# A two-layer decoder trunk on one core: half-size tiles for lone weight splits, and feed-forward down products accumulated onto the residual in PSUM

## The chip, the cores and the metric

The kernel runs on one core of one Trainium2 chip. The metric is the device time of one execution in microseconds (us). Three runs of the kernel before gave 2322.97, 2323.41 and 2323.65 us; the median is 2323.41 us.

## The reference, cut to what matters

The model is a trunk of two layers on 256 tokens of width 2048, in float32. Each layer has a token mixer beside a cross-attention, an output projection, and a SwiGLU feed-forward part (FFN) of inner width 5632. The change touches the FFN, the way in which weights are split for every projection, and the transposes.

```python
def ffn_part(h, layer):
    hn = _rmsnorm(h, norm_ffn[layer])
    gate, up = jnp.split(hn @ w_gate_up[layer], 2, axis=-1)
    h = h + (jax.nn.silu(gate) * up) @ w_down[layer]
    return h
```

## The kernel before, in words

Every float32 matrix product is made of three passes with rounded operands: each operand is split into a high part and a rest, and high x high, high x rest and rest x high are added in one PSUM bank. So every weight that arrives must be split by two instructions: ScalarE casts the high part (L207), VectorE subtracts it from the weight to get the rest (L208). `split` makes both, into a tile `parts` that holds two k-slices of 512 columns with their rests. There are six such tiles. The weights land in tiles `raw` of four slices of 128x512 (1 MB); there are four of these, given out in turn, so the load of `raw` number i waits until the last reader of number i-4 is through. All loads of weights are issued from SyncE's queue, in order.

Up and gate projection (`project_halves`, L321 to L372): the FFN width is worked off in 11 blocks of 512 columns. A block is made of eight pieces, each with one `raw` tile (two loads of 512 KB: columns of gate and of up). Most pieces (kind S) are a Strassen-like step: seven products in place of eight, for which VectorE forms sums of weight slices in place in `raw` (L350, L351, L352) before they are split. Kind S makes four splits: `a` is one slice alone, `b`, `c` and `d` are two slices each; `c` needs L350, `d` needs L351 and L352. Kind O makes two splits, `a` and `b`, of two slices each. From the fourth block of a layer the kinds are S S O S S O S S. The products of a block collect in seven of the eight PSUM banks, and VectorE adds these up (L833) and makes the gated value (L836).

Down projection (`down`, L843 to L853, with `project`, L220 to L254): blocks in pairs (the first alone) are multiplied with `w_down`, in four pieces of 512 output columns each; two such pieces are made behind each block, while the remainder of the queue `todo` waits. A down piece has one PSUM bank for each half of the tokens, and at its end `add_h` (L410 to L414) lets VectorE add both banks onto the residual `h`: two instructions, L414. The last part (blocks 9 and 10) follows at the layer's end with other work behind it.

The order of the instructions on each engine is fixed when the program is built, by a scheduler that starts from the order in the source, from free buffers and from its own estimate of durations. Each engine then works its list in order. The profile names weight tiles by their running number: pieces 160 to 167 are the eight pieces of block 7 in layer 0, and 156 to 159 are the down weights before them.

Of the kernel before, what the change touches and what calls it, by code (L numbers as in the profile page):

```python
# [35 lines left out]
def trunk_kernel(ctx: ExitStack, tc: tile.TileContext, x, mem, norm_mix, norm_ffn, norm_mem,  # L36
# [118 lines left out]
    def transposes(srcs, name):  # L155

        ps = aux_ps(name)
        for k, src in enumerate(srcs):
            for t in range(NT):
                nc.tensor.transpose(out=ps[:, k * T + t * P:k * T + (t + 1) * P], in_=src(t), identity=ident)  # L160
        return ps

    def make_quad(quad, src, gains, same=False):

# [31 lines left out]
    def new_raw():  # L196
        i = n_w[0]
        n_w[0] += 1
        return i, wts.tile([P, 4, 512], F32, tag="raw", name=f"raw{i}", bufs=4)

    def split(src, name, by=2):

        n, m = src.shape[1:]
        both = wts.tile([P, 2, 2, 512], F32R, tag="parts", name=f"parts{name}", bufs=6)
        for k in range(0, n, by):
            j = min(k + by, n)
            nc.scalar.copy(out=both[:, 0, k:j, 0:m], in_=src[:, k:j, :])  # L207
            nc.vector.tensor_tensor(out=both[:, 1, k:j, 0:m], in0=src[:, k:j, :],  # L208
                                    in1=both[:, 0, k:j, 0:m].bitcast(F32), op=ALU.subtract)
        return [(both[:, 0, k, 0:m], both[:, 1, k, 0:m]) for k in range(n)]  # L210
# [6 lines left out]
                              in_=w[(k0 + j) * P:(k0 + j + m) * P, c0:c0 + n].rearrange("(k p) c -> p k c", p=P))  # L217
        return [p for k in range(0, nk, 2) for p in split(raw[:, k:k + 2, 0:n], f"{i}_{k}", 1 if i == 0 else 2)]

    def project(quads, order, w, c0, n, name, parts=None, prep=None, by_tile=None):  # L220

        parts = parts or [(0, n)]
        ps = [[mm_ps(f"{name}_{i}_{t}") for t in range(NT)] for i in range(len(parts))]
        if by_tile is None:
            groups = [([qi], range(NT)) for qi in range(len(order))]
        else:
            groups = [(range(len(order)), [t]) for t in range(NT)]  # L230
        got = {}
        for qis, ts in groups:
            for qi in qis:
                q = order[qi]
                if prep:
                    prep(q)
                if qi not in got:
                    got[qi] = weights(w, 4 * q, 4, c0, n)
                for k, (hi, lo) in enumerate(got[qi]):
                    if k == 2 or (k == 0 and qi > 0):  # L240
                        step()
                    first = qi == 0 and k == 0
                    last = qi == len(order) - 1 and k == 3
                    for t in ts:
                        xh = quads[q].h[:, k, t * P:(t + 1) * P]
                        xl = quads[q].l[:, k, t * P:(t + 1) * P]
                        for i, (o, m) in enumerate(parts):
                            acc = ps[i][t][:, 0:m]
                            nc.tensor.matmul(acc, xh, hi[:, o:o + m], start=first, stop=False)  # L249
                            nc.tensor.matmul(acc, xh, lo[:, o:o + m], start=False, stop=False)  # L250
                            nc.tensor.matmul(acc, xl, hi[:, o:o + m], start=False, stop=last)  # L251
            if by_tile is not None:
                by_tile(ts[0], ps[0][ts[0]])
        return ps if len(parts) > 1 else ps[0]  # L254
# [66 lines left out]
    def project_halves(forms, kinds, w, c0, c1, name):  # L321
# [15 lines left out]
        for p, kind in enumerate(kinds):  # L337
# [4 lines left out]
                                  in_=w[2 * p * P:(2 * p + 2) * P, c:c + 512].rearrange("(k p) c -> p k c", p=P))  # L342
            x = forms[p].get
            last = p == len(PAIRS) - 1
            if kind == "S":
                tt = nc.vector.tensor_tensor
                b00, = split(raw[:, 0:1, :], f"{i}a")
                b11, b10 = split(raw[:, 2:4, :], f"{i}b")

                tt(out=raw[:, 0:2, :], in0=raw[:, 0:4:2, :], in1=raw[:, 1:2, :].broadcast_to([P, 2, 512]), op=ALU.subtract)  # L350
                tt(out=raw[:, 2, :], in0=raw[:, 2, :], in1=raw[:, 0, :], op=ALU.add)  # L351
# [36 lines left out]
    def h_forms(forms, n, gain, ss, name):  # L388

        for t in range(NT):  # L390
            square_sum(h[:, t, n * 512:(n + 1) * 512], ss[:, t, n:n + 1], f"{name}{n}{t}")

        def turn(p):
            forms[p] = Forms(p, f"{name}{p}")
            ps = aux_ps(f"tp_{name}{p}")
            for i, (t, k) in enumerate(((1, 0), (0, 0), (0, 1), (1, 1))):
                c = (2 * p + k) * P
                nc.tensor.transpose(out=ps[:, i * P:(i + 1) * P], in_=h[:, t, c:c + P], identity=ident)
            forms[p].put(ps, [gain[:, 2 * p + k:2 * p + k + 1] for k in range(2)])

        later(lambda: turn(2 * n), lambda: turn(2 * n + 1))
# [420 lines left out]
    def ffn(l, forms, r, after, tail=None):  # L822
# [21 lines left out]
        def down(i, n):  # L844
            end = i == len(PARTS) - 1
            if end and n == NQ - 1 and tail:
                flush()
                project(sq, PARTS[i], w_down[l], 512 * n, 512, f"fd{l}_{i}_{n}", by_tile=tail)
                return
            ps = project(sq, PARTS[i], w_down[l], 512 * n, 512, f"fd{l}_{i}_{n}")  # L850
            add_h(ps, 512 * n, 512)
            if end:
                after(n)  # L853

        todo = []
        for b in range(DFF // 512):
# [101 lines left out]
```

## Time and profile before

| | |
|---|---|
| median of three runs | 2323.41 us |
| the profiled execution's own time | 2322.12 us |
| its span, first to last instruction | 2320.3 us |
| TensorE busy (modelled ends) | 2297.6 us, 99% |
| VectorE busy | 1887.7 us, 81% |
| ScalarE busy | 1261.2 us, 54% |
| weights and other data read | 430.48 MB |

The shares are averages over stages. In the mixers (the first 520 us, and again from about 1220 to 1600 us) VectorE is busy 50 to 70% of the time; in the two FFN stages it is busy 99%. Matmuls overlap in this profile, and their ends are modelled, so TensorE's busy share says little; the spacing of their starts tells more.

### The profile page before, as it was taken

The page shows a single profiled execution, that of the slowest core. Times are in us where ns is not written, and L with a number is a line of the kernel's source. Part 1 is how long each engine was busy: PE and PEld are TensorE (multiplying, and loading weights), DVE is VectorE, ACT ScalarE, POOL GpSimd, SP SyncE. Part 2 cuts the span into 40 slices and gives each one's busy share as a digit, 9 for nine tenths or more (in the row PEclk, how much of TensorE's full clock was granted, in tenths as well). Part 3 has the DMA queues.
Part 4 walks back from the last instruction along what each step waited for, and adds up shares of the span by engine and source line. Part 5 has one row for each costly group of instructions (what it writes and reads, how often), then busy time and mean ns, then how long its engine had stood idle before and what let it go on. Part 6 is the DMA issues. An engine that isn't in the chain of part 4 may idle for free.

```text
span 2320.3 us, 28901 instructions
## 1 busy us (share of the span) xinstructions
PE 2297.6 (99%) x11034; PEld 1934.7 (83%) x11034; DVE 1887.7 (81%) x2262; ACT 1261.2 (54%) x1643; POOL 22.2 (1%) x39
## 2 busy tenths in 40 slices
PE   9999999999999999999999999999999999999998
PEld 7888888888887888888889999988887888888886
DVE  5566565668999999999985665567999999999995
ACT  7543534455555555555555654455555555555563
POOL 0000000000000000000000000000000000000000
PEclk9999999999999999999999999999999999999999
DMA  8554545455556556566565445555555556656563
GB/s 316 192 172 162 164 150 176 145 182 176 186 188 212 200 188 205 189 209 208 183 226 167 150 150 167 161 199 164 178 203 198 201 187 210 202 189 210 200 217 127
DMA packets 229211, 435.51 MB, mean 188 GB/s; under 512 B 10028, under 2 KB 38992, under 8 KB 228816
## 3 DMA queue, kind: packets, MB, share of 16 engines
q1 hardware_dynamic: 227776, 429.40, 55.5%
q10 hardware_dynamic: 1296, 4.26, 0.5%
q8 instruction: 86, 1.41, 0.2%
q14 instruction: 53, 0.43, 0.1%
HBM read 430.48 MB, written 3.15 MB: 187 GB/s over the span
## 4 chain that ended last, share of the span: by engine, by line
PE 63%; DVE 25%; issue 6%; ACT 4%; DMA 0%; ACTq 0%; DVEq 0%; POOLq 0%; SPq 0%
PE f_p L334 5%; PE f_p L335 5%; PE f_p L333 4%; DVE raw L350 4%; DVE parts L208 4%; PE fd L250 3%; PE fd L249 3%; PE fd L251 3%; PE wo L251 3%; PE wo L249 3%; PE wo L250 3%; DVE raw L351 2%; DVE raw L352 2%; PE hgate L249 1%; PE gv L249 1%
## 5 line engine op out<-in xcount | busy, mean ns | idle before, releaser
L208 DVE TENSOR_TENSOR parts<-raw,parts 128x1024 fp32r<-128x1024 f32 (+3 forms) x490 | 557.7, 1147 | 289.1 <-ACT parts L207 288.2
L207 ACT CAST parts<-raw 128x1024 fp32r<-128x1024 f32 (+3 forms) x490 | 476.8, 991 | 424.6 <-PE wo L251 64.4
L350 DVE TENSOR_TENSOR raw<-raw 128x1024 f32<-128x1024 f32 x118 | 143.6, 1217 | 0.2
L351 DVE TENSOR_TENSOR raw<-raw 128x512 f32<-128x512 f32 x118 | 81.6, 692 | 3.9
L352 DVE TENSOR_TENSOR raw<-raw 128x512 f32<-128x512 f32 x118 | 81.6, 692 | 3.8
L414 DVE TENSOR_TENSOR h<-fd,h 128x512 f32<-128x512 f32 x94 | 61.9, 684 | 6.2 <-PE fd L251 6.1
L833 DVE TENSOR_TENSOR e<-f_p,e 128x512 f32<-128x512 f32 x66 | 44.9, 680 | 0.0
L835 ACT ACTIVATE s<-s,rf_r 128x512 f32<-128x512 f32 x44 | 31.8, 722 | 6.9 <-DVE s L833 6.9
L836 DVE SCALAR_TENSOR_TENSOR s<-e,rf_r,s 128x512 f32<-128x512 f32 x44 | 32.3, 742 | 0.0
L562 DVE COPY_PREDICATED sch<-mask,slh 96x512 f32<-96x512 uint8 (+3 forms) x15 | 10.8, 721 | 25.1 <-PE slh L578 25.1
L833 DVE TENSOR_TENSOR s<-f_p,e 128x512 f32<-128x512 f32 x44 | 29.5, 682 | 0.0
L578 PEld LDWEIGHTS slh<-Q,K 128*96 128x96 f32 (+3 forms) x240 | 25.4, 176 | 1.4
L249 PE MATMUL wo<-parts,y_3h 128*128 128x512 f32 x64 | 25.9, 405 | 0.0
L249 PE MATMUL wo<-parts,y_0h 128*128 128x512 f32 x64 | 25.7, 402 | 0.0
L250 PE MATMUL fd<-parts,s_3h 128*128 128x512 f32 x64 | 25.4, 396 | 0.0
L249 PE MATMUL fd<-parts,s_0h 128*128 128x512 f32 x64 | 25.3, 396 | 0.0
L249 PE MATMUL fd<-parts,s_2h 128*128 128x512 f32 x64 | 25.3, 396 | 0.0
L249 PE MATMUL fd<-parts,s_6h 128*128 128x512 f32 x64 | 25.3, 396 | 0.0
L249 PE MATMUL fd<-parts,s_4h 128*128 128x512 f32 x64 | 25.3, 396 | 0.0
L250 PE MATMUL fd<-parts,s_5h 128*128 128x512 f32 x64 | 25.3, 396 | 0.0
L249 PE MATMUL fd<-parts,s_8h 128*128 128x512 f32 x64 | 25.3, 396 | 0.0
L250 PE MATMUL fd<-parts,s_0h 128*128 128x512 f32 x64 | 25.3, 396 | 0.0
(5486 smaller groups left out, 7396.4 us busy)
## 6 DMA issues: line engine op xcount, KB each, us to landing
raw<-in_w_gate_up_dram SPq DMA_DIRECT2D x352, 512.0 KB, 4.0
raw<-in_w_down_dram SPq DMA_DIRECT2D x88, 1024.0 KB, 5.0
raw<-in_hgrn_w_in_dram SPq DMA_DIRECT2D x52, 1024.0 KB, 5.0
raw<-in_gla_w_in_dram SPq DMA_DIRECT2D x48, 768.0 KB, 4.3
raw<-in_w_out_dram SPq DMA_DIRECT2D x32, 1024.0 KB, 4.9
raw<-in_w_mem_kv_dram SPq DMA_DIRECT2D x15, 1024.0 KB, 8.2
raw<-in_gla_w_in_dram SPq DMA_DIRECT2D x8, 528.0 KB, 3.7
mtok<-in_mem_dram SPq DMA_DIRECT2D x4, 512.0 KB
```

The source lines that it names most:

```text
L207: nc.scalar.copy(out=both[:, 0, k:j, 0:m], in_=src[:, k:j, :])
L208: nc.vector.tensor_tensor(out=both[:, 1, k:j, 0:m], in0=src[:, k:j, :], in1=both[:, 0, k:j, 0:m].bitcast(F32), op=ALU.subtract)
L249: nc.tensor.matmul(acc, xh, hi[:, o:o + m], start=first, stop=False)
L250: nc.tensor.matmul(acc, xh, lo[:, o:o + m], start=False, stop=False)
L251: nc.tensor.matmul(acc, xl, hi[:, o:o + m], start=False, stop=last)
L333: nc.tensor.matmul(ps[b], xh, hi, start=first, stop=False)
L334: nc.tensor.matmul(ps[b], xh, lo, start=False, stop=False)
L335: nc.tensor.matmul(ps[b], xl, hi, start=False, stop=left[b] == 0)
L350: tt(out=raw[:, 0:2, :], in0=raw[:, 0:4:2, :], in1=raw[:, 1:2, :].broadcast_to([P, 2, 512]), op=ALU.subtract)
L351: tt(out=raw[:, 2, :], in0=raw[:, 2, :], in1=raw[:, 0, :], op=ALU.add)
L352: tt(out=raw[:, 3, :], in0=raw[:, 3, :], in1=raw[:, 2, :], op=ALU.subtract)
L833: nc.vector.tensor_tensor(out=out, in0=ps[p], in1=q, op=ALU.add)
```

## The change

There are four edits.

- `split` takes a half-size tile (tag `part`, two of them) where one slice is split alone, instead of a full `parts` tile. To make room, there are three `raw` tiles instead of four.
- A down piece that is not in the last part no longer ends in two VectorE additions. Before its first matmul ScalarE copies the residual's two halves into the two PSUM banks (L247), the matmuls accumulate onto them, and ScalarE copies the sums back to `h` (L235).
- The copy back is late: `held` keeps it until `give_back` is called, which is behind the splits of the next weights (in `project`), or behind the second split of a piece S (in `project_halves`, from the second piece).
- The four transposes that share one PSUM bank are written with the flag that begins a group on the first alone, where each had it.

```diff
@@ transposes
-        for k, src in enumerate(srcs):
-            for t in range(NT):
-                nc.tensor.transpose(out=ps[:, k * T + t * P:k * T + (t + 1) * P], in_=src(t), identity=ident)
+        turns(ps, [src(t) for src in srcs for t in range(NT)])
         return ps
+
+    def turns(ps, srcs):
+        for i, src in enumerate(srcs):
+            nc.tensor.matmul(ps[:, i * P:(i + 1) * P], src, ident, start=i == 0, stop=i == len(srcs) - 1,
+                             is_transpose=True, skip_group_check=True)
@@ new_raw, split
-        return i, wts.tile([P, 4, 512], F32, tag="raw", name=f"raw{i}", bufs=4)
+        return i, wts.tile([P, 4, 512], F32, tag="raw", name=f"raw{i}", bufs=3)
...
-        both = wts.tile([P, 2, 2, 512], F32R, tag="parts", name=f"parts{name}", bufs=6)
+        if n == 1:
+            both = wts.tile([P, 2, 1, 512], F32R, tag="part", name=f"parts{name}", bufs=2)
+        else:
+            both = wts.tile([P, 2, 2, 512], F32R, tag="parts", name=f"parts{name}", bufs=6)
@@ project
+    held = []
+
+    def give_back():
+        while held:
+            hs, ps = held.pop(0)
+            for t in range(NT):
+                nc.scalar.copy(out=hs[:, t, :], in_=ps[t])
...
+        if onto:
+            for t in range(NT):
+                nc.scalar.copy(out=ps[0][t], in_=onto(t))
...
                     got[qi] = weights(w, 4 * q, 4, c0, n)
+                    give_back()
...
-                    first = qi == 0 and k == 0
+                    first = qi == 0 and k == 0 and not onto
@@ project_halves
+            if kind != "S":
+                give_back()
             if kind == "S":
                 tt = nc.vector.tensor_tensor
                 b00, = split(raw[:, 0:1, :], f"{i}a")
                 b11, b10 = split(raw[:, 2:4, :], f"{i}b")
+                if p > 0:
+                    give_back()
@@ down
-            ps = project(sq, PARTS[i], w_down[l], 512 * n, 512, f"fd{l}_{i}_{n}")
-            add_h(ps, 512 * n, 512)
             if end:
+                ps = project(sq, PARTS[i], w_down[l], 512 * n, 512, f"fd{l}_{i}_{n}")
+                add_h(ps, 512 * n, 512)
                 after(n)
+                return
+            hs = h[:, :, 512 * n:512 * n + 512]
+            ps = project(sq, PARTS[i], w_down[l], 512 * n, 512, f"fd{l}_{i}_{n}", onto=lambda t: hs[:, t, :])
+            held.append((hs, ps))
```

The edits also move instructions. In the changed file the split's cast and subtraction are L215 and L216, the sums of weight slices L377 to L379, the addition of the products L858. Three places follow.

**VectorE, the middle of block 7 in layer 0.** The names are those of pieces 160 to 163 (`parts163a` is split `a` of piece 163, `raw163` its weights, `fd0_2_3` the second down piece before the block). The order before:

```order
L208 TENSOR_TENSOR parts160d_7050<-raw160_7035,parts160d_7050 128x1024
L414 TENSOR_TENSOR h_87<-fd0_2_3_0_0_6967,h_87 128x512
L414 TENSOR_TENSOR h_87<-fd0_2_3_0_1_6968,h_87 128x512
L208 TENSOR_TENSOR parts161a_7084<-raw161_7081,parts161a_7084 128x512
L208 TENSOR_TENSOR parts161b_7087<-raw161_7081,parts161b_7087 128x1024
L350 TENSOR_TENSOR raw161_7081<-raw161_7081 128x1024
L351 TENSOR_TENSOR raw161_7081<-raw161_7081 128x512
L352 TENSOR_TENSOR raw161_7081<-raw161_7081 128x512
L208 TENSOR_TENSOR parts161c_7093<-raw161_7081,parts161c_7093 128x1024
L208 TENSOR_TENSOR parts161d_7096<-raw161_7081,parts161d_7096 128x1024
L208 TENSOR_TENSOR parts162a_7123<-raw162_7120,parts162a_7123 128x1024
```

And the order of the change from the same split on:

```order
L216 TENSOR_TENSOR parts160d_7072<-raw160_7057,parts160d_7072 128x1024
L216 TENSOR_TENSOR parts161b_7109<-raw161_7103,parts161b_7109 128x1024
L378 TENSOR_TENSOR raw161_7103<-raw161_7103 128x512
L216 TENSOR_TENSOR parts161c_7117<-raw161_7103,parts161c_7117 128x1024
L379 TENSOR_TENSOR raw161_7103<-raw161_7103 128x512
L216 TENSOR_TENSOR parts163a_7180<-raw163_7177,parts163a_7180 128x512
L216 TENSOR_TENSOR parts161d_7120<-raw161_7103,parts161d_7120 128x1024
L216 TENSOR_TENSOR parts162a_7147<-raw162_7144,parts162a_7147 128x1024
L216 TENSOR_TENSOR parts162b_7150<-raw162_7144,parts162b_7150 128x1024
L216 TENSOR_TENSOR parts163b_7183<-raw163_7177,parts163b_7183 128x1024
L377 TENSOR_TENSOR raw163_7177<-raw163_7177 128x1024
```

The two additions are gone, and the lone split `a` of the next S piece has moved up: 161a and L377 of 161 stand ahead of these rows, and 163a stands ahead of 161d and of both splits of piece 162.

**VectorE, the end of the same block.** Before, with `s0_7<-f0_7_p2` the first addition of the block's products:

```order
L350 TENSOR_TENSOR raw167_7303<-raw167_7303 128x1024
L351 TENSOR_TENSOR raw167_7303<-raw167_7303 128x512
L352 TENSOR_TENSOR raw167_7303<-raw167_7303 128x512
L208 TENSOR_TENSOR parts167c_7315<-raw167_7303,parts167c_7315 128x1024
L833 TENSOR_TENSOR s0_7_7343<-f0_7_p2_7061,e0_7_7342 128x512
L208 TENSOR_TENSOR parts167d_7318<-raw167_7303,parts167d_7318 128x1024
```

Now:

```order
L216 TENSOR_TENSOR parts166d_7303<-raw166_7288,parts166d_7303 128x1024
L216 TENSOR_TENSOR parts167b_7333<-raw167_7327,parts167b_7333 128x1024
L216 TENSOR_TENSOR parts167c_7339<-raw167_7327,parts167c_7339 128x1024
L378 TENSOR_TENSOR raw167_7327<-raw167_7327 128x512
L379 TENSOR_TENSOR raw167_7327<-raw167_7327 128x512
L216 TENSOR_TENSOR parts167d_7342<-raw167_7327,parts167d_7342 128x1024
L858 TENSOR_TENSOR s0_7_7367<-f0_7_p2_7083,e0_7_7366 128x512
```

Split 167d now stands right behind L379, which makes what it splits; before, two instructions stood between.

**ScalarE, from the down pieces into block 7, in the changed kernel** (COPY at L247 fills a bank from `h`, COPY at L235 is a copy back):

```order
L247 COPY fd0_2_3_0_0_6987<-h_87 128x512
L247 COPY fd0_2_3_0_1_6988<-h_87 128x512
L215 CAST parts159_2_7030<-raw159_7025 128x1024
...
L215 CAST parts160d_7072<-raw160_7057 128x1024
L215 CAST parts161b_7109<-raw161_7103 128x1024
L235 COPY h_87<-fd0_2_3_0_0_6987 128x512
L215 CAST parts161c_7117<-raw161_7103 128x1024
L235 COPY h_87<-fd0_2_3_0_1_6988 128x512
L215 CAST parts163a_7180<-raw163_7177 128x512
L215 CAST parts161d_7120<-raw161_7103 128x1024
L215 CAST parts162a_7147<-raw162_7144 128x1024
```

ScalarE had none of these copies; the casts of 161c, 163a and 161d now stand behind copies back that wait for the end of the down piece on TensorE, and the cast of 161d stands behind that of 163a.

## Rows read from the trace of the kernel before

**Rows 1.** The page: busy us (share of span) and instructions of each engine.
```profile
PE 2297.6 (99%) x11034; PEld 1934.7 (83%) x11034; DVE 1887.7 (81%) x2262; ACT 1261.2 (54%) x1643; POOL 22.2 (1%) x39
```

**Rows 2.** Windows: length, busy us and count by engine, PEclk, DMA share, GB/s.
```profile
0.00:58.00 58.00, 52.47 (x241) 43.02 (x242) 32.90 (x48) 41.31 (x76) 2.52 (x9) 1.00 0.87 316
464.00:522.00 58.00, 58.00 (x267) 47.96 (x266) 36.01 (x44) 32.71 (x46) 0.00 (x0) 1.00 0.57 182
...
918.61:981.76 63.15, 62.91 (x279) 51.16 (x278) 62.44 (x70) 36.09 (x42) 0.00 (x0) 1.00 0.61 200
...
671.40:728.90 57.50, 56.30 (x251) 45.65 (x249) 56.85 (x65) 31.31 (x38) 0.00 (x0) 1.00 0.59 199
```

**Rows 3.** Timeline of TensorE, piece 153: start us, us, line, tiles, count.
```profile
906.84 0.39 PE L333 MATMUL f_p<-parts153a,hf_5h 128*128 128x512 f32 x1
...
912.28 0.39 PE L333 MATMUL f_p<-parts154a,hf_6hl 128*128 128x512 f32 x1
```

**Rows 4.** Timeline of VectorE, one piece S of block 6.
```profile
907.84 0.68 DVE L208 TENSOR_TENSOR parts154a<-raw,parts154a 128x512 fp32r<-128x512 f32 x1
...
909.58 1.22 DVE L350 TENSOR_TENSOR raw<-raw 128x1024 f32<-128x1024 f32 x1
910.83 0.69 DVE L351 TENSOR_TENSOR raw<-raw 128x512 f32<-128x512 f32 x1
911.55 0.69 DVE L352 TENSOR_TENSOR raw<-raw 128x512 f32<-128x512 f32 x1
912.16 1.22 DVE L208 TENSOR_TENSOR parts154c<-raw,parts154c 128x1024 fp32r<-128x1024 f32 x1
913.45 1.23 DVE L208 TENSOR_TENSOR parts154d<-raw,parts154d 128x1024 fp32r<-128x1024 f32 x1
914.59 0.68 DVE L208 TENSOR_TENSOR parts155a<-raw,parts155a 128x512 fp32r<-128x512 f32 x1
```

**Rows 5.** Timeline of VectorE, the additions of both down pieces and what follows.
```profile
934.71 1.27 DVE L414 TENSOR_TENSOR h<-fd,h 128x512 f32<-128x512 f32 x2
935.90 2.35 DVE L208 TENSOR_TENSOR parts<-raw,parts 128x1024 fp32r<-128x1024 f32 x2
...
944.95 1.37 DVE L414 TENSOR_TENSOR h<-fd,h 128x512 f32<-128x512 f32 x2
946.23 0.68 DVE L208 TENSOR_TENSOR parts161a<-raw,parts161a 128x512 fp32r<-128x512 f32 x1
```

**Rows 6.** Timeline of VectorE in an earlier block: a split right behind L350.
```profile
576.43 1.23 DVE L350 TENSOR_TENSOR raw<-raw 128x1024 f32<-128x1024 f32 x1
577.57 1.22 DVE L208 TENSOR_TENSOR parts92b<-raw,parts92b 128x1024 fp32r<-128x1024 f32 x1
```

**Rows 7.** Timeline of ScalarE: a copy out of PSUM, and casts of two slices and one.
```profile
918.61 0.58 ACT L830 COPY e<-f_p 128x512 f32<-128x512 f32 x1
919.09 1.06 ACT L207 CAST parts155d<-raw 128x1024 fp32r<-128x1024 f32 x1
...
943.64 0.61 ACT L207 CAST parts161a<-raw 128x512 fp32r<-128x512 f32 x1
```

**Rows 8.** Timelines: VectorE's split 163d, and SyncE's issue of the load behind it.
```profile
960.85 1.23 DVE L208 TENSOR_TENSOR parts163d<-raw,parts163d 128x1024 fp32r<-128x1024 f32 x1
...
962.11 0.37 SPq L341 DMA_DIRECT2D raw<-in_w_gate_up_dram  x1
```

**Rows 9.** Two loads of 512 KB, each alone in its window: issue, then us to landing.
```profile
L341 SPq DMA_DIRECT2D raw<-in_w_gate_up_dram x1: 368/368/368, 1088.4 to 1088.4; - x1
...
DMA to landing us min/median/max: 3.7/3.7/3.7
...
L341 SPq DMA_DIRECT2D raw<-in_w_gate_up_dram x1: 368/368/368, 1018.5 to 1018.5; - x1
...
DMA to landing us min/median/max: 5.3/5.3/5.3
```

**Rows 10.** Timeline of TensorE: the first matmul of piece 160, behind the last down piece.
```profile
945.43 0.39 PE L333 MATMUL f_p<-parts160a,hf_0h 128*128 128x512 f32 x1
```

More of the change, by code (lines that the diff above doesn't have):

```diff
@@ L218, in weights, with project @@
         return [p for k in range(0, nk, 2) for p in split(raw[:, k:k + 2, 0:n], f"{i}_{k}", 1 if i == 0 else 2)]
-    def project(quads, order, w, c0, n, name, parts=None, prep=None, by_tile=None):
+    held = []
[4 more added lines that the diff above has]
+                nc.scalar.copy(out=hs[:, t, :], in_=ps[t])
+    def project(quads, order, w, c0, n, name, parts=None, prep=None, by_tile=None, onto=None):
         parts = parts or [(0, n)]
         ps = [[mm_ps(f"{name}_{i}_{t}") for t in range(NT)] for i in range(len(parts))]
+        if onto:
+            for t in range(NT):
+                nc.scalar.copy(out=ps[0][t], in_=onto(t))
         if by_tile is None:
@@ L248, in project @@
                             acc = ps[i][t][:, 0:m]
-                            nc.tensor.matmul(acc, xh, hi[:, o:o + m], start=first, stop=False)
-                            nc.tensor.matmul(acc, xh, lo[:, o:o + m], start=False, stop=False)
-                            nc.tensor.matmul(acc, xl, hi[:, o:o + m], start=False, stop=last)
+                            free = dict(skip_group_check=True) if onto else {}
+                            nc.tensor.matmul(acc, xh, hi[:, o:o + m], start=first, stop=False, **free)
+                            nc.tensor.matmul(acc, xh, lo[:, o:o + m], start=False, stop=False, **free)
+                            nc.tensor.matmul(acc, xl, hi[:, o:o + m], start=False, stop=last, **free)
             if by_tile is not None:
@@ L395, in turn @@
             ps = aux_ps(f"tp_{name}{p}")
-            for i, (t, k) in enumerate(((1, 0), (0, 0), (0, 1), (1, 1))):
-                c = (2 * p + k) * P
-                nc.tensor.transpose(out=ps[:, i * P:(i + 1) * P], in_=h[:, t, c:c + P], identity=ident)
+            turns(ps, [h[:, t, (2 * p + k) * P:(2 * p + k + 1) * P] for t, k in ((1, 0), (0, 0), (0, 1), (1, 1))])
             forms[p].put(ps, [gain[:, 2 * p + k:2 * p + k + 1] for k in range(2)])
```

## The prediction, made before the changed kernel ran

> **What bounds the kernel now.** I read the page first. TensorE is busy 99% and VectorE 81% of the span [rows 1], but neither says which engine a stage waits for, so I took the windows next [rows 2]. In a mixer stretch TensorE is busy 58.00 of 58.00 us and VectorE 36.01: TensorE is the bound. In a block of the FFN (918.61 to 981.76, from one block's first product copy to the next) VectorE is busy 62.44 of 63.15 us. TensorE's own need follows from the spacing of its starts: the 24 matmuls of piece 153 go from 906.84 to 912.28, so 0.227 us each [rows 3]. A full block has 174 matmuls for up and gate, 96 for two down pieces and 8 short transposes (some 0.8 us): 270 x 0.227 + 0.8 = 62.1 us. So in the FFN's full blocks VectorE sets the pace, and TensorE would set it only 1.05 us sooner. That is the first thing to see: **whatever VectorE is relieved of, a block cannot fall below about 62.1 us.** There are 8 such intervals in each layer (one with small down pieces, 57.50 us, VectorE busy 56.85 [rows 2]), 16 in all. The ceiling of the gain is 16 x 1.05 = 17 us, 0.7% of the time.
>
> **The change, part by part,** for one full block.
>
> *Additions removed.* Four L414 go. From the first pair's start to the next instruction is 1.19 us, for the second pair 1.28 [rows 5]. All of it lies on VectorE's path: **-2.47 us**.
>
> *Copies added on ScalarE.* Four fill a bank, four copy back. A copy out of PSUM takes 0.58 us, and the next instruction starts 0.48 behind it [rows 7]; no row shows ScalarE writing PSUM, and I take the same, between nothing and the 0.61 of a cast within SBUF [rows 7]. 8 x 0.5 = 4 us more on an engine that is busy 36.09 of 63.15 us [rows 2]: it fits. What matters is whom they hold up. The fills stand well ahead of the matmuls that need them. The copy back of the second down piece waits for TensorE's end of that piece and stands ahead of the cast of 161c. TensorE goes on to piece 160 at 945.43 [rows 10], so that half of the piece is done by about 945.0, and the copy (0.5) and cast (1.06) end at about 946.6. VectorE without its additions comes to 161c at about 946.5 (160d starts 1.14 ahead of the additions of rows 5, at 943.8; 161b and L378 follow). So this costs 0 to 0.3 us, and the wait for weights that comes next in VectorE's list swallows it: **0**. If ScalarE were 1 us later, it would cost nothing still; from there on it would cost all.
>
> *Order on VectorE.* A split of two slices normally takes 1.14 us from start to start, a piece of one slice 0.6. In a piece S, L350 to L351 takes 1.25 and L351 to L352 0.72, because each reads what the one before wrote: 0.11 lost twice. Split d starts 1.90 behind L352, of which split c covers 1.14: d's cast on ScalarE must wait for L352 (0.15 lost) [rows 4]. With another instruction behind L350 the spacing is 1.14 [rows 6]. The half tiles let the scheduler pull in the next piece's a or L377 there. Before, six pieces lose 6 x 0.22 + 5 x 0.15 = 2.07 (the last has L833 ahead of d). In the new order I count 0.14 for piece 160, 0.11 for 161 (L378 behind 161b overwrites what it reads), 0.11, 0.11 and 0.13 for 163, 164 and 166. For 167 it is 0.11 and, as d stands right behind L379, 1.90 - 0.61 = 1.29. Sum 1.99: **-0.1**. The Trainium skill (VectorE: DVE Perf Modes, The DRAIN you can't avoid) says that the next vector instruction does not start before the pipe is empty and that chaining without semaphores doesn't avoid it; by that rule the order of instructions would fill no gap, and the interval would come out 1.1 us longer than I sum it. Rows 4 and 6 speak against it: 1.25 against 1.14 behind the same instruction.
>
> *Three raw tiles.* This is the price. The weights of piece 163 now take the buffer of 160, not of 159, so their load is issued when VectorE is through with 160d: 1.22 behind that split's start, and 0.03 for SyncE [rows 8]. The first half lands 3.7 us after issue where no load was issued shortly before, 5.3 where another went out 2.3 us ahead [rows 9]; here more than 6 us lie between, so I take 3.75. Handing over to ScalarE some 0.1, cast 0.61 [rows 7], over to VectorE 0.03. So 163a is ready 5.75 us after 160d's start. In VectorE's list only 160d, 161b, L378, 161c and L379 stand between: 3 x 1.14 + 0.11 + 2 x 0.61 = 4.75. **VectorE waits 1.0 us** for a split that nobody needs yet. Then 161d: ScalarE, in order, casts it behind 163a, until about 6.70, and VectorE would be there at 6.35: 0.35 more. The same stands at 166a (buffer of 163; between are three splits of two slices, 0.72 and 0.61, so 4.75 again): 1.0, and 0.38 for 164d. At 164a and 167a four such splits and an L377 stand between, 5.70 against 5.75: 0.05 each. 160a and 161a are far behind the release. Sum **+2.83**. Both ends: with landings 0.2 sooner than the shortest of rows 9 each of the two large waits loses 0.2, sum 2.4; with 5.3 everywhere four loads add 1.55 each, sum 9.0.
>
> *Other stages.* In each layer's second interval (also VectorE's, without additions) one such pair of waits appears: +1 each, 2 in all. At the start the load of raw 3 waits for the splits of raw 0, some 3 us later than now; but the queue is full there (316 GB/s in the first 58 us [rows 2]), so I take 1, between 0 and 3. The transposes are the same matmuls in the same number: 0, and nothing else would hide them. In the mixers VectorE and ScalarE are a third idle and splits wait for tiles, not loads: 0.
>
> **Sum.** One block: -2.47 - 0.08 + 2.83 = +0.28 us; 16 x 0.28 = 4.5; with 2 and 1: **+7.5 us**. The profiled execution took 2322.12 us (span 2320.3), which gives 2329.6; the median of the runs lies 1.3 higher. I forecast **2330 us**: VectorE gives up two adds and buys waits for weights.
>
> **The rivals.** (1) *TensorE's floor: faster.* If the first halves come 1 us sooner against VectorE's list than I count, the two large waits are gone, a block is at 63.15 - 2.47 - 0.1 + 0.8 = 61.4, below 62.1, and TensorE sets the pace: 16 x -1.05 = -17, some **2307 us**. For it: VectorE's busy sum alone would allow it, and 2.57 us less on it is more than the 1.05 that TensorE leaves. Against: the wait hangs on VectorE's own split, so it cannot be outrun. The floor is reached when the waits fall from 2.83 to 1.5 together, that is from 1.0 to 0.35 at each of the two places. (2) *No change.* With the waits at 2.4 in place of 2.8 the sum per block is -0.2 and the rest +3: **2323 us**. Nothing in the rows parts this from my forecast but 0.25 us in a landing. (3) *Slow loads or ScalarE behind.* With landings of 4.5 us, half way to 5.3, each of four waits grows by 0.75: +3 per block, **2378 us**; with 4.0, **2346**. For it: rows 9 show 5.3. Against: only behind a load issued just before. (4) *The skill's drain rule* as above: 16 x 1.1 more, **2348 us**; rows 6 are against it.
>
> **How the numbers follow.** A measurement of this kernel can tell about 0.2%, 4.7 us, from no change. Chances: my forecast (2328 to 2338) 0.32; no change (2319 to 2328) 0.29; faster 0.25, more than the rows alone give it, as a list of this length worked by hand may be off by 0.5 us per block on either side; slow loads 0.12; drain rule 0.02. So faster 0.25, same 0.29, slower 0.46. The range, 8 in 10, takes in most of (1) and the 4.0 us of (3): 2309 to 2347 us.
>
> **What would show it.** Right: in the FFN windows VectorE's busy time falls by about 2.5 us per block while the block stays at 63 to 64 us, and VectorE idles 1 us ahead of splits like 163a and 166a, behind ScalarE's cast, which waits for a load of gate and up weights, and 1.3 us ahead of 167d. Wrong: blocks near 62.1 us with VectorE idle but TensorE without gaps (rival 1); ScalarE's casts waiting for the down products and TensorE waiting for them (the copies cost after all); or landings away from 3.7 us.

## The result and the profile after

The changed kernel took 2328.22 us (median of 8 runs, 2326.58 to 2330.91), the kernel before 2322.98 us (median of 8, 2322.36 to 2323.65) on the same chip. The ratio is 1.0023, with a 95% interval of 1.0012 to 1.0034: a little slower, 5 us, where 7 had been forecast. The runs of the changed kernel lie 4.3 us apart, those of the kernel before 1.3; the experiments come back to that. The profiled execution took 2327.4 us, with a span of 2325.6.

The page's first part, in answer to [rows 1]:

```profile
PE 2289.7 (98%) x11034; PEld 1937.6 (83%) x11034; DVE 1833.6 (79%) x2182; ACT 1341.0 (58%) x1803; POOL 22.3 (1%) x39
```

VectorE has 80 instructions fewer and 54 us less to do, ScalarE 160 more and 80 us more. The kernel is still slower, so VectorE's work was not all that set its pace. The windows of four stretches of layer 0, each from one block's first product copy to the next, answer to [rows 2] (columns as there): the second interval, the fourth, a quiet full block (no waits but those named below, and short) and the block of pieces 160 to 167.

```profile
574.72:617.20 42.48, 42.48 (x193) 35.14 (x192) 40.94 (x47) 25.78 (x32) 0.00 (x0) 1.00 0.54 175
...
669.24:727.92 58.68, 57.52 (x258) 47.18 (x256) 54.05 (x60) 35.59 (x46) 0.00 (x0) 1.00 0.55 185
791.28:854.48 63.20, 62.43 (x278) 51.40 (x278) 59.63 (x65) 40.06 (x51) 0.00 (x0) 1.00 0.60 200
918.57:983.24 64.67, 62.91 (x278) 51.23 (x278) 59.63 (x65) 40.04 (x51) 0.00 (x0) 1.00 0.58 195
```

In a full block VectorE is busy 59.63 us where it was 62.44, and the block takes 63.20 to 64.98 us where it took 63.15 [rows 2]. VectorE idles now. Where, is told by its timeline in the block of the last row:

```profile
942.79 1.23 DVE L216 TENSOR_TENSOR parts160d<-raw,parts160d 128x1024 fp32r<-128x1024 f32 x1
...
945.79 1.22 DVE L216 TENSOR_TENSOR parts161c<-raw,parts161c 128x1024 fp32r<-128x1024 f32 x1
946.92 0.69 DVE L379 TENSOR_TENSOR raw<-raw 128x512 f32<-128x512 f32 x1
948.52 0.69 DVE L216 TENSOR_TENSOR parts163a<-raw,parts163a 128x512 fp32r<-128x512 f32 x1 [0.91 <-ACT parts163a L215]
949.47 1.23 DVE L216 TENSOR_TENSOR parts161d<-raw,parts161d 128x1024 fp32r<-128x1024 f32 x1 [0.26 <-ACT parts161d L215]
...
966.40 0.69 DVE L216 TENSOR_TENSOR parts166a<-raw,parts166a 128x512 fp32r<-128x512 f32 x1 [2.16 <-ACT parts166a L215]
967.35 1.23 DVE L216 TENSOR_TENSOR parts164d<-raw,parts164d 128x1024 fp32r<-128x1024 f32 x1 [0.25 <-ACT parts164d L215]
...
983.35 1.23 DVE L216 TENSOR_TENSOR parts167d<-raw,parts167d 128x1024 fp32r<-128x1024 f32 x1 [1.19 <-ACT parts167d L215]
```

There are the three places that the prediction named: the early splits 163a and 166a, each with a short wait at the d behind it, and 167d behind L379. TensorE feels VectorE's lateness at the block's end, at the first matmul with 167d. There it stood 0.22 us before, and 1.26 now:

```profile
983.36 0.51 PE L333 MATMUL f_p<-parts167d,hf_7h 128*128 128x512 f32 x1 [0.22 <-ACT parts167d L207]
```

```profile
983.37 0.50 PE L356 MATMUL f_p<-parts167d,hf_7h 128*128 128x512 f32 x1 [1.26 <-ACT parts167d L215]
```

ScalarE's timeline in the same stretch says what its casts wait for:

```profile
942.66 1.05 ACT L215 CAST parts161b<-raw 128x1024 fp32r<-128x1024 f32 x1
944.19 0.59 ACT L235 COPY h<-fd 128x512 f32<-128x512 f32 x1 [0.49 <-PE fd L274]
...
947.86 0.62 ACT L215 CAST parts163a<-raw 128x512 fp32r<-128x512 f32 x1 [1.64 <-DMA raw<-in_w_gate_up_dram]
...
965.75 0.62 ACT L215 CAST parts166a<-raw 128x512 fp32r<-128x512 f32 x1 [4.46 <-DMA raw<-in_w_gate_up_dram]
```

The copy back waits 0.49 for TensorE, and VectorE takes 161c without a wait: here the copies cost nothing. The cast of 163a waits for its weights. SyncE's view of that load, issued at 944.04, as VectorE is through with 160d:

```profile
L364 SPq DMA_DIRECT2D raw<-in_w_gate_up_dram x1: 367/367/367, 944.0 to 944.0; - x1
...
who waited for it (us, times):
  ACT parts163a L215: 1.6, 1
...
DMA to landing us min/median/max: 3.7/3.7/3.7
```

At 166a it is worse. 163d, whose buffer that load takes, starts at 959.41 and takes 1.23; the cast begins at 965.75, 5.1 us after its end, where 163's load needed 3.8 to the same point. SyncE issued that load at 960.67, 0.03 behind the split, so it is the landing that was late: the cast begins 5.08 us after issue, where it was 3.82 at 163a, though the issue before it lay over 7 us back.

### The profile page after: what moved, and what is told of

The parts are those of the page before. It is cut to its first block, busy times and chain, and to the rows that moved or that the text cites. A ratio compares the mean times of both kernels' runs of the same rounds, so it can differ in the third digit from the quotient of the medians.

```text
span 2325.6 us, 28876 instructions
## 1 busy us (share of the span) xinstructions
PE 2289.7 (98%) x11034; PEld 1937.6 (83%) x11034; DVE 1833.6 (79%) x2182; ACT 1341.0 (58%) x1803; POOL 22.3 (1%) x39
## 4 chain that ended last, share of the span: by engine, by line
PE 72%; DVE 13%; DMA 8%; ACT 5%; issue 2%; ACTq 0%; SPq 0%; POOLq 0%; DVEq 0%
DMA raw<-in_w_gate_up_dram 7%; PE f_p L356 6%; PE f_p L358 6%; PE f_p L357 6%; PE fd L274 5%; PE fd L273 5%; PE fd L272 5%; PE wo L272 3%; PE wo L274 3%; PE wo L273 3%; DVE raw L379 1%; DVE raw L378 1%; DVE parts L216 1%; PE hgate L272 1%; PE gv L272 1%
## 5 line engine op out<-in xcount | busy, mean ns | idle before, releaser
L216 DVE TENSOR_TENSOR parts<-raw,parts 128x1024 fp32r<-128x1024 f32 (+3 forms) x490 | 558.6, 1149 | 296.4 <-ACT parts L215 295.5
L215 ACT CAST parts<-raw 128x1024 fp32r<-128x1024 f32 (+3 forms) x490 | 480.7, 991 | 427.1 <-PE wo L274 63.8
L377 DVE TENSOR_TENSOR raw<-raw 128x1024 f32<-128x1024 f32 x118 | 143.8, 1219 | 0.1
L379 DVE TENSOR_TENSOR raw<-raw 128x512 f32<-128x512 f32 x118 | 81.2, 688 | 1.8
L235 ACT COPY h<-fd 128x512 f32<-128x512 f32 x80 | 45.5, 588 | 12.7 <-PE fd L274 11.9
L247 ACT COPY fd<-h 128x512 f32<-128x512 f32 x80 | 45.5, 584 | 1.7 <-DVE s_0l L149 1.6
L858 DVE TENSOR_TENSOR e<-f_p,e 128x512 f32<-128x512 f32 x66 | 45.1, 683 | 0.0
L860 ACT ACTIVATE s<-s,rf_r 128x512 f32<-128x512 f32 x44 | 31.9, 724 | 15.7 <-DVE s L858 15.7
L858 DVE TENSOR_TENSOR s<-f_p,e 128x512 f32<-128x512 f32 x44 | 29.8, 684 | 0.1
L274 PE MATMUL fd<-parts,s_2l 128*128 128x512 f32 x64 | 25.2, 394 | 0.0
```

The lines of the kernel that those rows point to most:

```text
L379: tt(out=raw[:, 3, :], in0=raw[:, 3, :], in1=raw[:, 2, :], op=ALU.subtract)
L858: nc.vector.tensor_tensor(out=out, in0=ps[p], in1=q, op=ALU.add)
```

## The experiments

Two theories stood against each other. Mine: VectorE gives up two pairs of additions and buys waits for weights, which come from three raw tiles together with split a standing early. The rival: the copies on ScalarE, which works in order, hold up casts and eat the gain. All ratios below are to the kernel before on the same chip, with 95% intervals; its medians there are 2322.95 to 2323.19 us, so the times can be compared with each other.

**The copies without the tiles** (`e1_onto_raw4`).

```diff
 # from the changed kernel
-  tag="raw", bufs=3
+  tag="raw", bufs=4
-        if n == 1:
-            both = wts.tile([P, 2, 1, 512], F32R, tag="part", name=f"parts{name}", bufs=2)
-        else:
-            both = wts.tile([P, 2, 2, 512], F32R, tag="parts", name=f"parts{name}", bufs=6)
+        both = wts.tile([P, 2, 2, 512], F32R, tag="parts", name=f"parts{name}", bufs=6)
```

> The change with its tiles put back: four raw tiles, six full parts tiles, no half tile; fills and copies back by ScalarE stay. Theory (VectorE gives up two pairs of additions and buys waits for weights with the three raw tiles and the early split a): without those waits VectorE needs 63.15 - 2.47 = 60.7 us per full block, TensorE's floor of 62.1 to 62.3 decides, and the first two intervals of each layer keep what they gained in the changed kernel (2.0 and 0.6 us). 16 x -0.9 - 5 = -20: 2303 us, 2298 to 2308. Rival (the copies on ScalarE hold up casts, so the down products on the residual are the price): no better than 2318 us, with casts waiting behind copies back.

Measured: 2341.88 us, 1.008 (1.0067 to 1.0094). My theory missed by 39 us, and the rival held. ScalarE's timeline behind the second down piece of the same block (L212 is the cast here, L232 the copy back), and VectorE's:

```profile
947.43 0.62 ACT L212 CAST parts161a<-raw 128x512 fp32r<-128x512 f32 x1 [1.25 <-PE fd L271]
949.48 0.59 ACT L232 COPY h<-fd 128x512 f32<-128x512 f32 x1 [1.43 <-PE fd L271]
950.10 1.05 ACT L212 CAST parts161b<-raw 128x1024 fp32r<-128x1024 f32 x1
```

```profile
948.08 0.69 DVE L213 TENSOR_TENSOR parts161a<-raw,parts161a 128x512 fp32r<-128x512 f32 x1 [0.65 <-ACT parts161a L212]
...
951.19 1.23 DVE L213 TENSOR_TENSOR parts161b<-raw,parts161b 128x1024 fp32r<-128x1024 f32 x1 [1.16 <-ACT parts161b L212]
...
956.05 1.23 DVE L213 TENSOR_TENSOR parts161d<-raw,parts161d 128x1024 fp32r<-128x1024 f32 x1 [1.17 <-ACT parts161d L212]
```

The cast of 161a is released by TensorE's down products. It reads nothing that they make, so what it waits for is a tile that they still read. The copy back behind it waits for the end of that down piece, and 161b stands behind the copy. VectorE sits idle through both. The wait at 161d is of another kind: its cast waits for the sum L376, which stands right ahead of it in VectorE's list. So the copies back are not free by themselves, though they are not all that this kernel pays for. In the changed kernel, 161a and 161b are cast before the copy back begins.

**The tiles without the copies** (`e2_half_adds`).

```diff
 # from the kernel before
-  tag="raw", bufs=4
+  tag="raw", bufs=3
+        if n == 1:
+            both = wts.tile([P, 2, 1, 512], F32R, tag="part", name=f"parts{name}", bufs=2)
...
```

> The tiles of the change alone: three raw tiles, half tiles for lone splits, but VectorE's additions onto the residual as before, nothing new on ScalarE. Theory: the waits at the early split a (0.9 each, two in a block, 0.26 behind each, 1.19 at the split behind L379) stand as in the changed kernel and the additions come on top: 2328 + 16 x 2.47 + 5 = 2373 us, less what the additions cover of the waits (they stand elsewhere in VectorE's list): 2350 to 2375. Rival (ScalarE's copies are what ate the gain in the changed kernel): 2318 to 2335 us.

Measured: 2361.64 us, 1.0167 (1.0153 to 1.0181), as my theory has it. VectorE waits at 163a and 161d as in the changed kernel, with the additions still in its list:

```profile
964.08 0.69 DVE L211 TENSOR_TENSOR parts163a<-raw,parts163a 128x512 fp32r<-128x512 f32 x1 [0.81 <-ACT parts163a L210]
965.03 1.23 DVE L211 TENSOR_TENSOR parts161d<-raw,parts161d 128x1024 fp32r<-128x1024 f32 x1 [0.25 <-ACT parts161d L210]
```

The four kernels make a table: neither half of the change 2323, the tiles alone 2361.6, the copies alone 2341.9, both 2328.2 us. Each half alone is slower than nothing; together they give back most of that. The copies are worth 33 us where the tiles are there, and cost 19 where they are not.

**Three raw tiles, full tiles only** (`e4_raw3_nopart`): the first experiment with `bufs=3` for raw.

> The change with three raw tiles but no half tiles: six full parts tiles serve lone splits too. VectorE's list then has 163a behind 162b, some 10 us behind 160d, against 5.75 us that the load and its cast need. Theory as first put (the wait comes from the load standing late against the early split a): no wait, TensorE's floor: 2303 us (2298 to 2310), like the kernel with four raw tiles. Rival (three raw tiles are the price by themselves, wherever split a stands, through loads that are issued late): 2318 to 2335 us.

Measured: 2340.33 us, 1.0073 (1.0059 to 1.0086). That is above both ranges, and the rival's cause is not there: four raw tiles gave 2341.88, so the fourth raw tile brings nothing here, and the time is lost as in the first experiment. What this was to show is shown by the next.

**Three raw tiles in the kernel before** (`e6_before_raw3`): one number, `bufs=4` to `bufs=3`, nothing else.

> The kernel before with three raw tiles and nothing else. In VectorE's list 163a stands some 12 us behind 160d there, and the load and its cast need 5.75. Theory (three raw tiles cost only where the lone split a has been moved up): 2323 us, within 4. Rival (a raw tile less costs by itself, since later loads reach ScalarE late anywhere): over 2330 us, with VectorE waiting for casts that wait for loads.

Measured: 2322.97 us, 1.0000 (0.9991 to 1.0008). A raw tile less costs nothing where no split stands early. With three raw tiles the waits for weights need the early split a as well.

**Seven full tiles instead of half tiles** (`e7_raw3_parts7`): from the kernel with three raw tiles and full tiles only, `bufs=6` to `bufs=7` for `parts`.

> Fills and copies back by ScalarE, three raw tiles, no half tiles, but seven full parts tiles in place of six (the room is that of the kernel before). Theory after the kernels with six full tiles (2340 to 2342 us): there the cast of 161a waits for TensorE to free one of six tiles, the copy back behind it waits for the end of the down piece, and 161b stands behind that; with a seventh tile the casts of 161a and 161b stand ahead of the copies back, and 163a is not moved up, so VectorE waits neither for casts nor for loads: 62.1 to 62.7 us per full block, 2300 to 2310. Rival (the copies back cost wherever they stand): 2330 or more.

Measured: 2314.14 us, 0.9962 (0.995 to 0.9975): 26 us less than with six tiles, some 4 above the range I gave. ScalarE's timeline shows the first copy back where the casts of 161a and 161b already lie behind it:

```profile
944.40 1.27 ACT L232 COPY h<-fd 128x512 f32<-128x512 f32 x2 [1.00 <-PE fd L271]
945.56 1.05 ACT L212 CAST parts161c<-raw 128x1024 fp32r<-128x1024 f32 x1
```

VectorE, which was to wait for nothing here, still waits, for 161b (whose cast waits 2.10 us for a tile that the down products still read) and for 161c (whose cast stands behind the copies):

```profile
943.43 1.23 DVE L213 TENSOR_TENSOR parts161b<-raw,parts161b 128x1024 fp32r<-128x1024 f32 x1 [1.17 <-ACT parts161b L212]
946.64 1.23 DVE L213 TENSOR_TENSOR parts161c<-raw,parts161c 128x1024 fp32r<-128x1024 f32 x1 [0.54 <-ACT parts161c L212]
```

In a block of this kernel TensorE is busy 62.65 of 62.80 us, so that waits of this size cost little. With six full tiles, VectorE's three waits at piece 161 came to 2.98 us and a block to 64.7. So what the copies back cost went with the number of tiles that the splits may run ahead; as the seventh tile also shortens the waits for a free tile, the two are not parted here.

**The room taken from the full tiles** (`e3_raw4_part2_parts5`).

```diff
 # from the changed kernel
-  tag="raw", bufs=3
+  tag="raw", bufs=4
-  tag="parts", bufs=6
+  tag="parts", bufs=5
```

> The change with the room taken elsewhere: four raw tiles and two half tiles, five full parts tiles in place of six. The early split a stays in VectorE's list, but its weights use the buffer of four pieces before, so they are long there. Theory: no wait for weights, TensorE's floor decides: 2303 us (2298 to 2310). Rival 1 (the order of VectorE's list is itself the price, as 163a stands ahead of 161d): 2320 or more. Rival 2: five parts tiles are too few, and splits wait for TensorE to free one: 2310 to 2330, with VectorE idle behind TensorE.

Measured: 2311.96 us, 0.9952 (0.9939 to 0.9964), 16 us less than the changed kernel. VectorE comes to 163a and doesn't wait:

```profile
944.49 1.23 DVE L216 TENSOR_TENSOR parts161c<-raw,parts161c 128x1024 fp32r<-128x1024 f32 x1 [0.54 <-ACT parts161c L215]
945.63 0.68 DVE L216 TENSOR_TENSOR parts163a<-raw,parts163a 128x512 fp32r<-128x512 f32 x1
```

It misses my range of 2298 to 2310 by 2 us, and the number lies in rival 2's. In a full block VectorE's waits still add up to 3.2 us, none of them for a load: 0.3 at 160b, 0.54 at 161c, whose cast stands behind the copies back, and 1.19 each at 163d and 167d, which stand right behind L379 in VectorE's list. TensorE is now busy 62.43 of 62.90 us, and what it still waits for stands at the block's last split. Its timeline there, with the start of the last matmul before the wait and of the one behind it 0.88 us apart:

```profile
1041.88 0.39 PE L356 MATMUL f_p<-parts179c,hf_7h 128*128 128x512 f32 x1
1042.76 0.50 PE L357 MATMUL f_p<-parts179d,hf_7h 128*128 128x512 f32 x1 [0.49 <-DVE parts179d L216]
```

**The last split in two** (`e8_last_d_by1`).

```diff
 # from the kernel with four raw, two half and five full tiles
-                t6, t4 = split(raw[:, 2:4, :], f"{i}d")
+                t6, t4 = split(raw[:, 2:4, :], f"{i}d", 1 if last else 2)
```

> The change with four raw, two half and five full tiles (2312 us), and in the last piece of a block split d is cast and subtracted slice by slice. Theory: in that kernel a block is 62.93 us, of which TensorE stands 0.88 at the last split, behind L379, and 62.05 is its floor. The slice that L379 doesn't make needs no wait, and the other's cast runs beside it: 0.5 to 0.9 us less in each of 20 blocks, 2294 to 2302 us. Rival (the wait is followed by another at the next down weights, or TensorE stands for another reason there): 2309 to 2314 us.

Measured: 2307.68 us, 0.9933 (0.992 to 0.9947). The direction is the theory's, the size is not: 4.3 us for 20 blocks, where 10 to 18 had been expected. The number lies between the theory's range and the rival's. VectorE now takes the slice that L379 doesn't make at once, and the other behind the next down weights:

```profile
975.63 0.69 DVE L379 TENSOR_TENSOR raw<-raw 128x512 f32<-128x512 f32 x1
976.36 0.69 DVE L216 TENSOR_TENSOR parts167d<-raw,parts167d 128x512 fp32r<-128x512 f32 x1
977.31 1.23 DVE L216 TENSOR_TENSOR parts<-raw,parts 128x1024 fp32r<-128x1024 f32 x1 [0.26 <-ACT parts L215]
978.46 0.68 DVE L216 TENSOR_TENSOR parts167d<-raw,parts167d 128x512 fp32r<-128x512 f32 x1
```

A window of one block shows VectorE far from the bound and TensorE at it (62.50 us long, TensorE busy 62.48, VectorE 59.44):

```profile
978.70:1041.20 62.50, 62.48 (x280) 51.26 (x279) 59.44 (x67) 40.42 (x51) 0.00 (x0) 1.00 0.60 202
```

This is the fastest version that was run, 15 us below the kernel before.

**The same edit on the change's own tiles** (`e10_after_d_by1`).

> The change with its own tiles (three raw, two half, six full), and in the last piece of a block split d is cast and subtracted slice by slice. The scheduler then also puts 161d ahead of 163a, and 163a some 5.9 us behind the start of 160d, where its load and cast need 5.75. Theory (the changed kernel pays for waits at 163a, 166a and 167d, by where they stand in VectorE's list): most of these waits go, and a block comes to 62.3 to 63.0 us: 2302 to 2314 us. Rival (with three raw tiles the loads are late anywhere): the wait moves to the next instruction that needs the load, 2320 us or more.

Measured: 2325.50 us, 1.0008 (0.9999 to 1.0017). My theory missed, and the time is the rival's. In the block of 920.84 to 984.6 VectorE no longer waits at 163a, but other waits are there: 0.93 us at 166a for its load as before, 1.18 at 161d, which now stands right behind L379, and 0.87 for a load of down weights. ScalarE casts those weights ahead of the silu (L860) that makes the second half of the gated value, VectorE waits for the silu, and TensorE's transposes of that half start 1.32 us behind the matmul before them:

```profile
929.07 1.05 ACT L215 CAST parts<-raw 128x1024 fp32r<-128x1024 f32 x1 [1.57 <-DMA raw<-in_w_down_dram]
930.02 0.72 ACT L860 ACTIVATE s<-s,rf_r 128x512 f32<-128x512 f32 x1
```

```profile
930.77 0.75 DVE L861 SCALAR_TENSOR_TENSOR s<-e,rf_r,s 128x512 f32<-128x512 f32 x1 [0.87 <-ACT s L860]
...
949.19 1.23 DVE L216 TENSOR_TENSOR parts161d<-raw,parts161d 128x1024 fp32r<-128x1024 f32 x1 [1.18 <-ACT parts161d L215]
...
965.42 0.69 DVE L216 TENSOR_TENSOR parts166a<-raw,parts166a 128x512 fp32r<-128x512 f32 x1 [0.93 <-ACT parts166a L215]
```

```profile
930.26 0.40 PE L274 MATMUL fd<-parts,s_4l 128*128 128x512 f32 x1
931.58 0.55 PE L165 MATMUL tp_s_6h<-ident,s 128*128 128x128 f32 x3 [0.93 <-DVE s L861]
```

So the rival's cause, loads that are late with three raw tiles, holds for two of the three waits; with four raw tiles (`e8_last_d_by1`) the same edit gave 2307.68 us.

**The first load cut in two** (`e13_slice0_first`): VectorE's list and all tiles stay near to the change, only the landing of the slice that split a needs comes sooner.

```diff
 # from the changed kernel
-            for j, c in ((slice(0, 4, 3), c0), (slice(1, 3), c1)):
-                nc.sync.dma_start(out=raw[:, j, :],
-                                  in_=w[2 * p * P:(2 * p + 2) * P, c:c + 512]...)
+            for j, k, m, c in ((slice(0, 1), 0, 1, c0), (slice(3, 4), 1, 1, c0), (slice(1, 3), 0, 2, c1)):
+                r0 = (2 * p + k) * P
+                nc.sync.dma_start(out=raw[:, j, :], in_=w[r0:r0 + m * P, c:c + 512]...)
```

> The change with the first load of a gate and up piece cut in two: the slice that split a needs goes out alone (256 KB), the other slice of the gate columns behind it, the up columns last. In VectorE's list 163a stands as far behind 160d as in the change (4.75 us of work). Theory (VectorE waits at 163a and 166a for the landing of that load, 3.72 us behind its issue in the changed kernel): the half of the bytes lands 0.2 to 0.8 us sooner, two waits in a block shrink by that, and ScalarE's cast behind them with it: 2304 to 2322 us. Rival 1 (the fixed part of a landing is nearly all of it): 2326 to 2330 us. Rival 2 (a third issue on SyncE, 0.37 to 0.41 us each, and more loads in flight make the other half late, which split b and the sums need): 2332 us or more.

Measured: 2310.44 us, 0.9945 (0.9931 to 0.9958): 18 us less than the changed kernel, by a load that lands sooner. This is the nearest that a run comes to the price of the waits: the same edits otherwise, the same bytes, and in VectorE's list, from 160d up to 163a, the same five instructions in another order (on ScalarE, 161c's cast now stands ahead of the copies back). The slice that split a needs lands 2.7 us after its issue, here that of 178a with no issue in the 6 us before it, where 512 KB took 3.7:

```profile
L365 SPq DMA_DIRECT2D raw<-in_w_gate_up_dram x1: 328/328/328, 1017.5 to 1017.5; - x1
...
DMA to landing us min/median/max: 2.7/2.7/2.7
```

And VectorE's wait at 163a is all but gone from its rows, with 0.36 us left at 161d:

```profile
942.73 0.69 DVE L216 TENSOR_TENSOR parts163a<-raw,parts163a 128x512 fp32r<-128x512 f32 x1
943.78 1.23 DVE L216 TENSOR_TENSOR parts161d<-raw,parts161d 128x1024 fp32r<-128x1024 f32 x1 [0.36 <-ACT parts161d L215]
```

Over the fourteen full blocks, VectorE's waits for casts that wait for gate and up weights fall from 1.7 us a block in the changed kernel to less than 0.1, and 16 of the 18 us lie in the sixteen intervals that the prediction summed. Its runs lie within 0.75 us of each other (5 runs), those of the changed kernel within 4.3 (8 runs). That fits a pace set by landings in the one and not in the other; no run tests the spread by itself.

**The half tiles with four raw tiles, additions kept** (`e9_half_adds_raw4`).

> Four raw, two half and five full tiles, with VectorE's additions onto the residual as before and no copies on ScalarE. Theory: VectorE still sets the pace, with the additions' 2.47 us in each full block, and gains only what the new order saves between dependent instructions (0 to 1 us): 62.5 to 63.3 us a block, 2312 to 2326 us, 2320 the likeliest. Rival 1 (the half tiles alone bring what the kernel with copies and these tiles has, so the copies are worth nothing): 2312 us or less. Rival 2 (five full tiles are too few without the copies' slack): over 2330.

Measured: 2351.80 us, 1.0124 (1.011 to 1.0138), which only rival 2 had, and not by its cause: VectorE doesn't wait for TensorE. A fourth raw tile doesn't end the waits here, because the scheduler moves split a up further: 178a stands ahead of 175d in VectorE's list, one piece earlier than with three raw tiles. ScalarE's cast of 178a waits for its load, and VectorE waits 1.26 us for the cast; as much again goes at each of 166d and 167d (1.20 and 1.19), which stand right behind the sum that makes what they split.

```profile
1034.22 0.62 ACT L210 CAST parts178a<-raw 128x512 fp32r<-128x512 f32 x1 [5.21 <-DMA raw<-in_w_gate_up_dram]
```

**The two small edits.** `e11_flags` is the kernel before with the flags of the transposes, `e12_after_prompt` the change with `give_back()` right behind `held.append((hs, ps))`.

> The kernel before with the transposes' flags of the change and nothing else. Theory: the same matmuls in the same number, 2323 us within 2. Rival (the four transposes of a bank run closer together or further apart): a change of the short gaps in TensorE by 0.1 to 0.3 us in each block, 2 to 6 us in all, to either side.

> The change with the copy back written right behind the down piece's matmuls. In ScalarE's list the copies stand at nearly the same places as in the change (one ahead of the cast of 160a, the others behind 161b as before), since the scheduler sets them. Theory: 2328 us within 4, the lateness in the source is worth nothing with these tiles. Rival (the copies now wait for TensorE ahead of casts that it needs next): 2335 us or more, with TensorE waiting at piece 160.

Measured: 2323.50 us, 1.0001 (0.9992 to 1.001), and 2328.03 us, 1.0020 (1.0011 to 1.0029). The flags are worth nothing in time. The second run is in effect the changed kernel again: on every engine the instructions stand in the same order in both, so the scheduler puts the copies where it will, and what a copy back would cost that really stands earlier is not shown. The Trainium skill (PSUM — Partial Sum Buffer, The four PSUM rules) says that a matmul with the flag that begins a group clears the bits that decide between adding and overwriting in its whole bank; no run here shows it.

## Why the prediction came out right, and where its steps failed

**The bound and the removed work: right.** VectorE set the pace, and its busy time fell by 2.81 us in a full block (62.44 to 59.63, overlaps not counted twice) against 2.47 counted from starts.

**The waits for weights: right in place and cause.** Forecast were 1.0 at 163a and at 166a, 0.35 and 0.38 at the d behind, 1.29 at 167d. In the quiet block of 791.28 the same places have waits of 0.82 and 0.79, 0.26 and 0.26, and 1.19. The forecast counts from start to start, and by that count each is 0.08 more, since an instruction that waits for nothing starts 0.08 ahead of the end of the one before. So the waits for weights come to some 2.45 us there, against 2.83. The load of 163 landed in 3.72 us, 3.75 taken. The experiments bear the cause out from four sides: nothing without the early split a (three raw tiles in the kernel before), the waits without the copies (tiles alone), no wait at 163a with a fourth raw tile and the copies, and 18 us less with a load that lands sooner.

**The term of 2.83 a block, with 3.75 us to landing everywhere, was too small on average.** The sixteen intervals from the fourth on grew by 0.76 us on average, not 0.28: 2.8 us for the two with small down pieces, 9.3 for the fourteen full ones. Quiet blocks have 63.2 to 63.4 us, as forecast, but others 63.6 to 65.0, through loads such as 166's that came 1.2 us later than counted (2.16 at 166a against 1.0). The prediction had that as its upper end and as rival 3, and the truth lies between that and the forecast. Its argument against rival 3, that a landing is late only behind a load issued just before, does not hold: 166's load landed late over 7 us behind the issue before it, and the load of rows 8 in the kernel before, 6.3 us behind its forerunner, had taken 5.0:

```profile
L341 SPq DMA_DIRECT2D raw<-in_w_gate_up_dram x1: 368/368/368, 962.1 to 962.1; - x1
...
DMA to landing us min/median/max: 5.0/5.0/5.0
```

**The term of +1 in each layer's second interval had the wrong sign.** A wait appears there, as forecast: 0.91 us at 98a and 0.26 at 96d. But the second and third interval together became 2.6 us shorter in each layer (44.48 and 52.62 us before, 42.48 and 52.04 after, in layer 0). Some of it is work that moved into the fourth interval (TensorE starts 193 matmuls in the second, before 197); the three together are 1.3 and 1.0 us shorter. I had counted only what VectorE waits for, not what TensorE no longer waits for: before, it lost 0.84 us at 96d, and now it has no such gap:

```profile
608.05 0.50 PE L333 MATMUL f_p<-parts96d,hf_4h 128*128 128x512 f32 x1 [0.68 <-ACT parts96d L207]
```

The kernels with six full tiles and no half tiles keep the 44.5 us; those with half tiles have 41.8 to 42.9, and the one with seven full tiles has 43.0. So this goes with the number of tiles that the splits may run ahead, and the half tiles are one way to it. So the sum of 7.5 us went wrong by +7.6 in the sixteen intervals (12.1 for 4.5), by -7.2 in the second and third (5.2 gained, where 2 had been counted as lost), by -0.6 at the start and by some -2 in the stages behind the blocks, whose cause no run shows. These nearly cancel, and the profiled executions are 5.3 us apart. That the total came so close is partly luck: two errors of over 7 us each have opposite signs.

**The term of 0 for the copies held for this change and was no property of the copies.** The step compared when ScalarE would be through with a copy back and when VectorE would want 161c, in the changed kernel's own order, and there it was right. With six full tiles and no half tiles the same edit of the down pieces cost 19 us.

**The rivals.** TensorE's floor was put at 62.1 us, and the fastest version's block of 62.50 us with TensorE busy 62.48 bears out that nothing much lies below. It was not reached here for the reason given: the waits for weights have to fall to 1.5 us a block, and they were 2.4 or more. The drain rule would have added 1.1 us to every block, a figure that the prediction gives without its working; the quiet blocks, 63.2 us where my sum says 63.43, leave no room for it. The section of the Trainium skill that the prediction cites for this rival (VectorE: DVE Perf Modes, The DRAIN you can't avoid) also says that a next instruction which is not held starts earlier, which the prediction left out. Rows 6 agree: the split starts 0.09 ahead of the end of the instruction before it.

## What to carry to other kernels

Before a buffer is taken from a ring of loads, look in the consuming engine's list for how much work stands between the instruction that frees the buffer and the one that needs the new load, and compare it with issue, landing and cast together (here 4.75 against 5.75 us); a ring may be one shorter at no cost (2323 us either way) until something lets the consumer ask sooner. Work that is moved to an engine with room still waits in that engine's order: a copy back that waits for TensorE costs what is queued behind it, and that was nothing, 0.5 or 1.2 us at a time, by how many tiles the queue had to run ahead. Two edits that each lose can hold each other up, so test them apart and together, and when one wait is taken away look for the next one.

## What the runs showed that was not expected

A load of half the size (256 KB for 512 KB), with the same bytes in all and some 0.36 us more of SyncE's issue time for each piece, landed 1.0 us sooner (2.7 against 3.7) and was worth 18 us over the kernel. The Trainium skill (DMA: Bandwidth & Descriptors, Rules for kernel authors) asks for at least 1 MiB per DMA where bandwidth is wanted. The loads of gate and up weights are below that already, and the run goes the other way: here an engine waits for the first bytes, the DMA engines are busy 0.61 of a block, and the smaller first load wins. ScalarE's copy into PSUM, which no row of before had, takes the same as a copy out of it: 0.584 us on average (80 copies at L247) against 0.588 (80 at L235).
